# A two-layer transformer trunk on one core: the opening's loads, its first norm factors and one more weight block are laid out anew

## The chip, the core and the metric

The kernel runs on one core of a Trainium2 chip. The metric is the device time of one execution in microseconds (us); lower is better. TensorE (PE in the rows) multiplies, VectorE (DVE), ScalarE (ACT) and GpSimd (POOL) do the rest, and SyncE (SP) issues nearly all DMAs, in one queue. Each engine works through its own instructions strictly in order and waits on semaphores for the others.

## What is computed

A token matrix `x` of 256 x 1024 goes through two layers of three parts: a gated feed-forward block (FFN), an attention mixer, a second FFN. Each part is wrapped in a norm whose shift, scale and gate come from a modulation row:

```python
c_act = jax.nn.silu(c)
mod = (c_act @ ada_w[l] + ada_b[l])[:, None, :]      # 1024 -> 9 x 1024, one row
h = rmsnorm(x, norm_pre[l, 0]) * (1.0 + sc1) + sh1
y = (jax.nn.silu(h @ w_gate) * (h @ w_up)) @ w_down  # 1024 -> 2816 -> 1024
x = x + 0.5 * g1 * rmsnorm(y, norm_post[l, 0])
```

All of it is float32. Of the modulation, the first FFN needs only the shift and scale (`sh1`, `sc1`, columns 0 to 2047 of `ada_w[0]`, 8 MB) before it can start.

## The kernel before

**Products.** Every float32 weight block (1 MB, 128 x 2048) is loaded into a `raw` buffer (3 of them), then split in `unit`: ACT writes the rounded `hi` (6 buffers), DVE writes `lo = raw - hi` (5 buffers), piece by piece; `split=4` makes pieces of 512 columns, `split=8` of 256. The activations are split in the same way into `hT[0]` and `hT[1]`. A product is then three matmuls: `hi*hi`, `hi*lo`, `lo*hi` (`mm3`, lines 487 to 489, 512 columns each; `mm2t`, lines 496 and 499, a pair of 512 and 256 columns).

**Stages.** A section is one FFN or one mixer; six follow each other, with a norm at each seam (`post_norm`, `pre_norm`). Within an FFN, `first` or two "solo" blocks give hidden columns 0 to 511; the loop over `j` (0 to 8) does 256 columns of gate and up at a time; `down` units (11) trail it by `lag`, and at least `tail` of them run behind the loop. Beside this runs the background modulation (`ada_part`, DVE line 524), 512 KB at a time, for later sections.

**The opening.** The first norm needs the modulation, so it is done by quarters q of 256 columns of `h`. For each q: two loads of `ada_w` (1 MB each, s = shift, c = scale, line 929), 16 narrow matmuls (line 991) into `parts`, the bias added on DVE (line 994), a matmul with `sel` that copies the row to all partitions (line 995), two DVE steps for each half of the tokens (lines 1003 and 1004, `gained` at 976 ahead of them), transposes (line 616) and the split of `h` (lines 619, 620). Then the `first` block of this quarter (gate and up columns 0 to 511, 1 MB) is multiplied: 24 matmuls of 512 columns. `START_ORDER` gives the order in which the loads are written: s and c the modulation, x the tokens, g the gain row of `norm_pre` (loaded 128 times over, 256 KB), f the first block. `warm` puts matmuls into the queue whose result is never read (line 969, four passes of 512 columns).

**Norm factors.** `rstd_of` takes the mean square from ACT and makes its inverse root on POOL in two steps: a sum with EPS (line 595) and a power (line 597).

**The order.** `keep_order` at the end models all instructions (costs, the gaps `READY`, priorities shifted by the `START_` and `SEC` numbers) and fixes the order on every engine. Its numbers set order only.

Of the kernel before, what the change touches and what calls it, by code (L numbers as in the profile page):

```python
# [29 lines left out]
START_MM, START_CONV, START_CHAIN, START_SMALL = 590, 826, -286, 74  # L30
START_ORDER = ['s0 x0 s1 c0 g0 x1 c1 f0 s2 f1', 'c2 g1 f2 s3 c3 f3', '', '', '']
WARM = [2, 5, 2]
SEC = [
    dict(plan=('3542', 20, 3), tail=1, lag=1, split=4, sum=-921, dma=-218),
    dict(plan=('76', 9, 4), mix='0011002103011010110011', split=4, sum=-57, dma=24),
    dict(plan=('a8b', 20, 5), tail=4, lag=-1, split=8, sum=353, dma=194),
    dict(plan=('4325', 30, 0), tail=3, lag=1, split=4, sum=-423, dma=-500),
    dict(plan=('67', 8, 3), mix='0000121030111011001011', split=4, sum=473, dma=-406),
    dict(plan=('8', 14, 1), tail=3, lag=2, split=4, sum=-97, dma=-346),
# [4 lines left out]
READY = {("SP", "DVE"): 3600, ("SP", "PE"): 3700, "SP": 3510, ("PE", "DVE"): 290, "PE": 200, ("DVE", "PE"): 235,  # L44
         "DVE": 200, ("Activation", "PE"): 275, "Activation": 145, "Pool": 60}
AFTER = {"SP": 0, "PE": 0, "DVE": 125, "Activation": 100, "Pool": 90}
FBI, BSLACK, FSLACK = 4, {'DVE': 60, 'Activation': 40}, {'DVE': 370, 'Activation': 810}
# [34 lines left out]
def keep_order(tc, nc, slots, shifts):  # L82
# [10 lines left out]
    dur = [cost(i, e, slots) for i, e in zip(L, eng)]  # L93
    prio = list(range(N))
# [60 lines left out]
    def forward(prio):  # L155
# [33 lines left out]
        for _ in range(10 * N):  # L189
# [50 lines left out]
            for j in succs[k]:  # L240
                npred[j] -= 1
                gap = AFTER[e] if eng[j] == e and not dma[k] else READY.get((e, eng[j]), READY[e])
                ready[j] = max(ready[j], end + gap if preds[j][k] else start)
                if not npred[j]:
                    offer(j)
# [7 lines left out]
    def backward(at_, reuse):  # L253
# [16 lines left out]
        while True:  # L270
# [8 lines left out]
            for j, kind in ps[k].items():  # L279
                nsucc[j] -= 1  # L280
                if kind is True:
                    gap = AFTER[eng[j]] if eng[j] == e and not dma[j] else READY.get((eng[j], e), READY[eng[j]])
                else:
# [23 lines left out]
def trunk(ctx, tc, x, c, rel_bias, ada_w, ada_b, norm_pre, norm_post, w_gate, w_up,  # L307
# [74 lines left out]
    nc.vector.memset(mhalf, -0.5)  # L382
    xs = [ctile([P, D], f"x{h}") for h in range(2)]
# [56 lines left out]
    def unit(key, shape, src, uses=1):  # L440

        if key not in units:
# [3 lines left out]
            for z in range(sec["split"]):  # L446
                sl = slice(z * 2048 // sec["split"], (z + 1) * 2048 // sec["split"])
                nc.scalar.activation(hi[:, sl], raw[:, sl], AF.Copy)  # L448
                nc.vector.tensor_sub(lo[:, sl], raw[:, sl], hi[:, sl].bitcast(F32))  # L449
            units[key] = [uses, hi.rearrange("p (a b) -> p a b", a=shape[0]),  # L450
                          lo.rearrange("p (a b) -> p a b", a=shape[0])]
# [233 lines left out]
    def ffn(l, i, first):  # L685
# [21 lines left out]
        for j in range(9):  # L707
# [4 lines left out]
            gu = []  # L712
            for b, (tag, ws) in enumerate((("g", w_gate), ("u", w_up))):
                w = u_both(l, f, ws, tag, j)
                gu.append(st())
                for t in range(2):
                    p_ = wps(b)
                    mm2t(p_, KT, w, slice(t * P, (t + 1) * P))
                    dst = gu[b][:, t * 256:(t + 1) * 256]
                    nc.scalar.activation(dst, p_[:, 256:], AF.Copy)  # L720
                    nc.vector.tensor_add(dst, p_[:, :256], dst)  # L721
            nc.scalar.activation(gu[0], gu[0], AF.Silu)
            nc.vector.tensor_mul(gu[0], gu[0], gu[1])
            act = split(gu[0], 512)
# [201 lines left out]
    def ada_load(m, q):  # L926

        raw = (plo if m else phi).tile([P, KT, 256], F32, tag="lo" if m else "hi", name=nm("eraw"))
        nc.sync.dma_start(raw, rows(ada_w[0], 0, KT)[:, :, m * D + q * 256:m * D + (q + 1) * 256])
        return raw  # L930
# [4 lines left out]
    def load_gain(n):  # L935
        grow[n] = stage()
        nc.sync.dma_start(grow[n], norm_pre[0, 0:1, n * 512:(n + 1) * 512].to_broadcast([P, 512]))

    def load_first(q):
        loaded["first", q] = load((4, 512), first_srcs(q))  # L940

# [16 lines left out]
    def start_load(order):  # L958
        for w in order.split():
            {"s": lambda q: load_mod(q, 0), "c": lambda q: load_mod(q, 1), "x": load_x, "g": load_gain,  # L960
             "f": load_first}[w[0]](int(w[1]))
# [8 lines left out]

    warm(WARM[0], gb)
    rx, xg = [None, None], [[None, None], [None, None]]
# [58 lines left out]
    keep_order(tc, nc, slots, shifts)  # L1031
# [48 lines left out]
```

## Time and profile before

| | |
|---|---|
| three runs, median (lowest to highest) | 1021.07 us (1020.7 to 1021.27) |
| profiled execution, its own time | 1020.83 us |
| its span in the profile | 1019.0 us |
| busy share of the span: PE, DVE, ACT, POOL | 98%, 84%, 59%, 4% |
| moved by DMA | 261.82 MB, 257 GB/s mean |

The 1.8 us between the profiled execution's time and its span lie outside the instructions. A matmul's "busy" time is longer than its share of the engine, since matmuls are pipelined; the distance from one start to the next is what one costs. `x16` on line 991 is 8 instructions: a float32 matmul has two records.

### The profile page before, as it was taken

What the parts mean: (1) busy time and instruction counts of PE and PEld (TensorE: products, weight loads), DVE (VectorE), ACT (ScalarE), POOL (GpSimd) and SP (SyncE); (2) the same over time, 40 slices, a digit from 0 to 9 for tenths busy, and PEclk for the clock granted to TensorE, in tenths of its full rate; (3) what the DMA queues carried; (4) which work ended last, traced back from release to release, by engine and by line L of the source; (5) the groups of instructions that cost most, each with busy time, mean ns of one, the idle gap of its engine ahead of it and who ended that gap; (6) DMA issues with size and microseconds to landing.
All of it is one profiled execution on the core that took longest, in us unless ns stands there. A gap on an engine that the chain in (4) does not pass through costs nothing. (4 is left out here: it accounts for less than half of the span.)

```text
span 1019.0 us, 15260 instructions
## 1 busy us (share of the span) xinstructions
PE 999.0 (98%) x5362; PEld 833.0 (82%) x5362; DVE 852.3 (84%) x1637; ACT 600.0 (59%) x1394; POOL 44.2 (4%) x92
## 2 busy tenths in 40 slices
PE   8999999999999999999999999999999999999997
PEld 3588888887888888888878888888888788888886
DVE  4799999988987998899789999987878898666652
ACT  3256555664677675667465566655477666655541
POOL 1000000011001000000020000000100110000000
PEclk9999999999999999999999999999999999999999
DMA  9999899857995588888549999977689747655511
GB/s 332 367 340 328 304 308 342 307 197 230 334 315 191 185 288 280 281 288 297 203 164 319 323 324 311 311 258 244 195 296 295 242 144 264 206 173 200 182 66 42
DMA packets 171848, 261.82 MB, mean 257 GB/s; under 512 B 6396, under 2 KB 107484, under 8 KB 171772
## 3 DMA queue, kind: packets, MB, share of 16 engines
q1 hardware_dynamic: 171616, 260.78, 75.9%
q8 instruction: 42, 0.69, 0.3%
q14 instruction: 34, 0.28, 0.1%
q10 hardware_dynamic: 156, 0.07, 0.0%
HBM read 259.76 MB, written 1.07 MB: 256 GB/s over the span
## 5 line engine op out<-in xcount | busy, mean ns | idle before, releaser
L449 DVE TENSOR_TENSOR lo_a<-raw_a,hi_a 128x512 fp32r<-128x512 f32 (+1 forms) x540 | 296.6, 593 | 37.1 <-PE w_b L499 10.8
L448 ACT ACTIVATE hi_a<-raw_a 128x512 fp32r<-128x512 f32 (+1 forms) x540 | 261.1, 548 | 52.6 <-DMA raw_a<-in_ffn_w_up_dram 16.2
L496 PE MATMUL w_a<-hT,hi_a 128*128 128x512 f32 x640 | 223.9, 397 | 0.0
L496 PE MATMUL w_b<-hT,hi_b 128*128 128x512 f32 x512 | 179.4, 397 | 0.0
L499 PE MATMUL w_a<-hT,lo_a 128*128 128x256 f32 x640 | 166.6, 281 | 0.0
L496 PEld LDWEIGHTS w_a<-hT,hi_a 128*128 128x128 f32 x640 | 116.7, 188 | 22.7 <-DVE str_a L660 0.2
L449 DVE TENSOR_TENSOR lo_b<-raw_b,hi_b 128x512 fp32r<-128x512 f32 (+1 forms) x224 | 121.0, 589 | 15.5 <-PE w_a L499 7.2
L499 PE MATMUL w_b<-hT,lo_b 128*128 128x256 f32 x512 | 132.9, 281 | 0.0
L499 PEld LDWEIGHTS w_a<-hT,lo_a 128*128 128x128 f32 x640 | 120.8, 189 | 7.1
L448 ACT ACTIVATE hi_b<-raw_b 128x512 fp32r<-128x512 f32 (+1 forms) x224 | 106.2, 544 | 20.8 <-DMA raw_b<-in_ffn_w_up_dram 7.6
L496 PEld LDWEIGHTS w_b<-hT,hi_b 128*128 128x128 f32 x512 | 93.7, 188 | 18.7 <-issue 0.6
L499 PEld LDWEIGHTS w_b<-hT,lo_b 128*128 128x128 f32 x512 | 96.6, 189 | 5.9
L524 DVE SCALAR_TENSOR_TENSOR acc_a<-araw_a,ccol,acc_a 128x512 f32<-128x512 f32 x110 | 82.2, 747 | 2.3 <-DMA araw_a<-in_ada_w_dram 0.7
L720 ACT ACTIVATE st_a<-w_a 128x256 f32<-128x256 f32 x80 | 30.4, 383 | 76.7 <-PE w_a L496 75.7
L720 ACT ACTIVATE st_b<-w_b 128x256 f32<-128x256 f32 x64 | 24.1, 384 | 64.1 <-PE w_b L496 63.8
L487 PE MATMUL a_b<-hi_a,str_a 128*128 128x512 f32 x156 | 60.9, 391 | 0.0
L488 PE MATMUL a_b<-lo_a,str_a 128*128 128x512 f32 x156 | 60.8, 391 | 0.0
L489 PE MATMUL a_b<-hi_a,str_a 128*128 128x512 f32 x156 | 60.4, 390 | 0.0
L721 DVE TENSOR_TENSOR st_a<-w_a,st_a 128x256 f32<-128x256 f32 x80 | 33.3, 421 | 16.6 <-ACT st_a L720 16.3
L595 POOL TENSOR_SCALAR rstd_a<-ss_a 128x1 f32<-128x1 f32 x13 | 6.6, 511 | 721.0 <-ACT junk L645 694.4
L487 PE MATMUL w_a<-hi_a,hT 128*128 128x512 f32 (+1 forms) x96 | 36.6, 381 | 0.6 <-DVE hT L620 0.6
L507 PE MATMUL w_a<-hT,hi_a 128*128 128x256 f32 x128 | 37.0, 292 | 0.0
(255 smaller groups left out, 1930.0 us busy)
## 6 DMA issues: line engine op xcount, KB each, us to landing
araw_a<-in_ada_w_dram SPq DMA_DIRECT2D x84, 512.0 KB
raw_a<-in_ffn_w_down_dram SPq DMA_DIRECT2D x30, 1024.0 KB
raw_a<-in_ffn_w_gate_dram SPq DMA_DIRECT2D x26, 1024.0 KB
raw_a<-in_ffn_w_up_dram SPq DMA_DIRECT2D x26, 1024.0 KB
araw_b<-in_ada_w_dram SPq DMA_DIRECT2D x44, 512.0 KB
raw_a<-in_mix_w_in_dram SPq DMA_DIRECT2D x18, 1024.0 KB
raw_b<-in_ffn_w_gate_dram SPq DMA_DIRECT2D x16, 1024.0 KB
raw_b<-in_ffn_w_up_dram SPq DMA_DIRECT2D x16, 1024.0 KB
```

What stands on the lines that cost most here:

```text
L448: nc.scalar.activation(hi[:, sl], raw[:, sl], AF.Copy)
L449: nc.vector.tensor_sub(lo[:, sl], raw[:, sl], hi[:, sl].bitcast(F32))
L487: nc.tensor.matmul(ps_, hh, wh, start=start, stop=False)
L488: nc.tensor.matmul(ps_, hh, wl, start=False, stop=False)
L489: nc.tensor.matmul(ps_, hl, wh, start=False, stop=stop)
L496: both = lambda **f: nc.tensor.matmul(ps_, wh, hTa[:, kt], **f)
L499: nc.tensor.matmul(ps_[:, :256], wl, hT[0][:, kt], start=False, stop=False)
L507: nc.tensor.matmul(ps_, wh, hh, start=start, stop=False)
L524: nc.vector.scalar_tensor_tensor(acc[:, :n], raw[:, t, :], ccol[:, k:k + 1], b if t == 0 else acc[:, :n], op0=ALU.mult, op1=ALU.add)
L595: nc.gpsimd.tensor_scalar(r, s0, 1.0 if s1 is None else s1, EPS, op0=ALU.mult if s1 is None else ALU.add, op1=ALU.add)
L720: nc.scalar.activation(dst, p_[:, 256:], AF.Copy)
L721: nc.vector.tensor_add(dst, p_[:, :256], dst)
```

## The change

- **Loads.** For the first quarter the shift and the scale columns come as two loads of 512 KB each. A new load b (`load_next`) brings, by quarters of 512 KB, the gate and up weights of the loop's block `j = 0`.
- **Products.** In each quarter 24 matmuls of 256 columns on this block stand with the first block's (lines 1057 to 1059), into PSUM tiles `ahead`; `ffn` then takes `j = 0` from there.
- **Bias and gain.** In quarter 0 the bias goes into `both` by a product of one row (line 1016), the two halves of `parts` are copied by ACT and DVE (line 1024) and spread apart (line 1025). The gain row is loaded once (2 KB, ACT's queue) and spread by a product of one row (line 957).
- **Norm factors.** `rstd_of` adds EPS and the two sums on ACT (lines 605, 608); the power stays on POOL (line 609).
- **Numbers.** The two last `warm` matmuls go; `lag`, `tail`, `split`, the plans of the background work and the planner's gaps change in most sections: `split` 4 to 8 in the fourth and fifth, `lag` 1 to 2 in the first and fourth, `tail` 4 to 5 in the third.

```diff
-START_ORDER = ['s0 x0 s1 c0 g0 x1 c1 f0 s2 f1', 'c2 g1 f2 s3 c3 f3', '', '', '']
-WARM = [2, 5, 2]
+START_ORDER = ['g0 x0 s0 c0 f0 x1 b0 s1 c1 f1 b1 g1 s2', 'c2 f2 b2 s3', 'c3 f3 b3', '', '']
+WARM = [2, 5, 0]
-    dict(plan=('3542', 20, 3), tail=1, lag=1, split=4, sum=-921, dma=-218),
+    dict(plan=('3542', 19, 6), tail=1, lag=2, split=4, sum=-921, dma=-218),
...
-    dict(plan=('4325', 30, 0), tail=3, lag=1, split=4, sum=-423, dma=-500),
-    dict(plan=('67', 8, 3), mix='0000121030111011001011', split=4, sum=473, dma=-406),
+    dict(plan=('4325', 31, 1), tail=3, lag=2, split=8, sum=-859, dma=-502),
+    dict(plan=('67', 9, 4), mix='0000121030111011001011', split=8, sum=680, dma=-406),
...
-        r, r2 = tiny(1, tag), tiny(1, tag + "2")
-        nc.gpsimd.tensor_scalar(r, s0, 1.0 if s1 is None else s1, EPS, op0=ALU.mult if s1 is None else ALU.add,
-                                op1=ALU.add)
-        nc.gpsimd.tensor_tensor(r2, r, mhalf, op=ALU.pow)
-        return r2
+        r = tiny(1, tag)
+        e = eps
+        if s1 is not None:
+            e = tiny(1, tag + "e")
+            nc.scalar.activation(e, s0, AF.Identity, bias=eps)
+            s0 = s1
+        v = tiny(1, tag + "v")
+        nc.scalar.activation(v, s0, AF.Identity, bias=e)
+        nc.gpsimd.tensor_tensor(r, v, mhalf, op=ALU.pow)
+        return r
...
+            if q == 0:
+                nc.tensor.matmul(both, sel[0:1, :], fl(brow0[0:1, 0]), start=True, stop=False)
...
+                if q == 0:
+                    (nc.vector.tensor_copy if z else nc.scalar.copy)(t[:, zc], parts[:, zc])
+                    nc.tensor.matmul(both[:, zc], sel, t[:, zc], start=False, stop=z == 1)
...
+        with shift(START_CONV):
+            w = unit(("next", q), (4, 256), None, 1)
+        with shift(START_NEXT):
+            for n in range(2):
+                for t in range(2):
+                    for k in range(2):
...
+                        nc.tensor.matmul(p_, wh, hT[0][:, kt], start=kt == t == 0, stop=False)
+                        nc.tensor.matmul(p_, wh, hT[1][:, kt], start=False, stop=False)
+                        nc.tensor.matmul(p_, wl, hT[0][:, kt], start=False, stop=kt == 7 and t == 1)
```

Three places show how instructions move. First, TensorE in the first quarter, before (`a_b` is the filler's target, `eraw` a modulation block, `x_120` the second half of the tokens):

```order
L969 MATMUL a_b_137<-x_119,ident 128x512 x4
L991 MATMUL w_a_202<-eraw_a_147,ccol 32x256 x8
L991 MATMUL w_a_202<-eraw_a_152,ccol 32x256 x8
L995 MATMUL w_a_203<-st_a_220,str_a_138 128x512
L969 MATMUL a_b_137<-x_120,ident 128x512
L616 MATMUL w_a_226<-ident,st_a_223 128x128
L991 MATMUL w_a_289<-eraw_a_150,ccol 32x256 x6
```

and after:

```order
L1021 MATMUL w_a_224<-eraw_a_155,ccol 32x256 x4
L1016 MATMUL w_a_225<-erow_a_146,str_a_140 128x512
L1021 MATMUL w_a_224<-eraw_a_158,ccol 32x256 x8
L1025 MATMUL w_a_225<-st_a_226,str_a_140 128x256
L994 MATMUL a_b_139<-x_121,ident 128x512
L1025 MATMUL w_a_225<-st_a_226,str_a_140 128x256
```

The filler on `x_120` ahead of the first transpose is gone, and no matmul of quarter 1 stands between the two transposes of quarter 0 any more; fillers on `x_121`, the first half of the tokens, stand between the pieces.

Second, SyncE's queue at the start, before:

```order
L933 DMA x_119<-in_x_dram 128x1024
L929 DMA eraw_a_152<-in_ada_w_dram 128x8x256
L929 DMA eraw_a_147<-in_ada_w_dram 128x8x256
L929 DMA eraw_a_150<-in_ada_w_dram 128x8x256
L937 DMA str_a_154<-in_norm_pre_dram 128x512
L933 DMA x_120<-in_x_dram 128x1024
L437 DMA raw_a_159<-in_ffn_w_gate_dram 128x2x512
L929 DMA eraw_a_157<-in_ada_w_dram 128x8x256
```

and after:

```order
L951 DMA x_121<-in_x_dram 128x1024
L947 DMA eraw_a_158<-in_ada_w_dram 128x4x256
L947 DMA eraw_a_155<-in_ada_w_dram 128x4x256 x2
L947 DMA eraw_a_158<-in_ada_w_dram 128x4x256
L951 DMA x_122<-in_x_dram 128x1024
L443 DMA raw_a_161<-in_ffn_w_gate_dram 128x2x512
L443 DMA raw_a_165<-in_ffn_w_gate_dram 128x2x256
L443 DMA raw_a_161<-in_ffn_w_up_dram 128x2x512
L443 DMA raw_a_165<-in_ffn_w_up_dram 128x2x256
```

The first quarter's two blocks come in four pieces, the second half of the tokens and the first blocks stand ahead of the second quarter's modulation, and `raw_a_165` is the new block.

Third, TensorE in quarter 2, from the spreading matmul (line 995) to the transposes (line 616), before:

```order
L995 MATMUL w_a_361<-st_a_378,str_a_138 128x512
L489 MATMUL a_b_137<-hi_a_318,hT 128x512
L616 MATMUL w_a_386<-ident,st_a_383 128x128 x2
L991 MATMUL w_a_435<-eraw_a_282,ccol 32x256 x8
L487 MATMUL a_a_134<-hi_a_391,hT 128x512
```

and after (line 1028 spreads, line 628 transposes):

```order
L1028 MATMUL w_a_458<-st_a_459,str_a_140 128x512
L1059 MATMUL w_a_198<-hT,lo_a_416 128x256
L496 MATMUL a_a_137<-hi_a_373,hT 128x512
L494 MATMUL a_b_138<-hi_a_373,hT 128x512
L495 MATMUL a_b_138<-lo_a_374,hT 128x512
L496 MATMUL a_b_138<-hi_a_373,hT 128x512
```

One product stood there before; ten stand there now (one of 256 and nine of 512 columns), of which the first five are shown.

## Rows read from the trace of the kernel before

**Rows 1.** Windows: busy us (and instructions) by engine, granted clock, DMA share, GB/s.

```profile
core 0: us, PE busy (x) PEld busy (x) DVE busy (x) ACT busy (x) POOL busy (x), PEclk, DMA share, GB/s
0.00:10.00 10.00, 7.34 (x14) 3.27 (x15) 2.71 (x6) 2.92 (x6) 2.63 (x13) 1.00 0.83 276
10.00:20.00 10.00, 8.03 (x54) 2.78 (x55) 4.31 (x8) 1.97 (x6) 0.87 (x2) 0.83 1.08 366
20.00:30.00 10.00, 10.00 (x62) 6.45 (x64) 6.96 (x15) 4.12 (x9) 0.00 (x0) 1.00 1.07 376
30.00:40.00 10.00, 8.86 (x58) 5.20 (x50) 7.64 (x12) 2.30 (x4) 0.00 (x0) 1.00 1.09 358
40.00:50.00 10.00, 9.10 (x62) 5.38 (x61) 8.31 (x17) 3.71 (x7) 0.00 (x0) 1.00 1.07 370
...
60.00:222.00 162.00, 162.00 (x841) 137.34 (x840) 153.56 (x258) 98.54 (x200) 1.60 (x3) 1.00 0.93 319
524.00:712.00 188.00, 187.34 (x963) 158.53 (x962) 172.95 (x287) 107.70 (x216) 4.74 (x8) 1.00 0.85 289
```

**Rows 2.** Timeline, first quarter: start, busy us, engine, line, idle before and its releaser.

```profile
7.13 3.70 PE L969 MATMUL a_b<-x,ident 128*128 128x512 f32 x8
...
13.79 1.10 PE L995 MATMUL w_a<-st_a,str_a 128*128 128x512 f32 x2 [0.90 <-DVE st_a L994]
...
19.99 0.38 ACT L619 ACTIVATE hT<-w_a 128x256 fp32r<-128x256 f32 x1 [2.12 <-PE w_a L616]
...
21.00 0.79 PE L487 MATMUL a_a<-hi_a,hT 128*128 128x512 f32 x1
```

**Rows 3.** Timeline: paces of PE: eight of line 991, then 512 and 256 columns.

```profile
22.17 1.07 PE L991 MATMUL w_a<-eraw_a,ccol 128*32 128x256 f32 x16
...
23.17 0.50 PE L487 MATMUL a_b<-hi_a,hT 128*128 128x512 f32 x1
...
25.98 0.39 PE L488 MATMUL a_a<-lo_a,hT 128*128 128x512 f32 x1
...
26.89 0.39 PE L488 MATMUL a_a<-lo_a,hT 128*128 128x512 f32 x1
...
226.49 0.28 PE L487 MATMUL w_a<-hi_a,hT 128*128 128x256 f32 x1
...
226.97 0.28 PE L488 MATMUL w_a<-lo_a,hT 128*128 128x256 f32 x1
```

**Rows 4.** Timeline, quarter 2: the step on DVE and the transposes behind it.

```profile
40.54 0.42 DVE L1004 TENSOR_TENSOR st_a<-st_a,w_a 128x256 f32<-128x256 f32 x1
...
41.11 0.41 PE L616 MATMUL w_a<-ident,st_a 128*128 128x128 f32 x2 [0.83 <-DVE st_a L1004]
```

**Rows 5.** Timeline: the first block's last matmul, then block 0 of the loop.

```profile
56.56 0.39 PE L489 MATMUL a_b<-hi_a,hT 128*128 128x512 f32 x1
...
57.58 0.40 PE L496 MATMUL w_a<-hT,hi_a 128*128 128x512 f32 x1
...
57.93 0.40 PE L496 MATMUL w_a<-hT,hi_a 128*128 128x512 f32 x1
...
59.73 0.66 PE L682 MATMUL w_b<-ident,st_b 128*128 128x128 f32 x4 [0.70 <-DVE st_b L666]
```

**Rows 6.** Groups by line and form, DVE: the low parts of the weights.

```profile
L449 DVE TENSOR_TENSOR lo_a<-raw_a,hi_a 128x512 fp32r<-128x512 f32 x356 | 229.3, 684 | 32.7 <-PE w_a L499 9.8 <-PE w_b L499 8.6 <-ACT hi_a L448 7.9
L449 DVE TENSOR_TENSOR lo_a<-raw_a,hi_a 128x256 fp32r<-128x256 f32 x184 | 67.3, 417 | 4.5 <-PE w_b L499 2.2 <-ACT hi_a L448 2.0
```

**Rows 7.** Groups by form: POOL's norm factors, a tiny ACT step; timeline: a seam.

```profile
L595 POOL TENSOR_SCALAR rstd_b<-ss_b 128x1 f32<-128x1 f32 x11 | 7.4, 670 | 34.2 <-ACT junk L645 23.9 <-ACT junk L625 7.9 <-DVE st_b L635 2.2
L597 POOL TENSOR_TENSOR rstd_b<-rstd_b,mhalf 128x1 f32<-128x1 f32 x11 | 6.3, 576 | 0.8
L414 ACT ACTIVATE bq<-w_b 128x8 f32<-128x8 f32 x1 | 0.2, 178 | 0.2 <-PE w_b L412 0.2
...
230.89 0.33 PE L750 MATMUL w_a<-ident,st_a 128*128 128x128 f32 x1 [1.36 <-DVE st_a L797]
```

More of the change, by code (lines that the diff above doesn't have):

```diff
@@ L93, in keep_order @@
     dur = [cost(i, e, slots) for i, e in zip(L, eng)]
+    lag = [LATE[k >= at[calm]] if d else 0 for k, d in enumerate(dma)]
     prio = list(range(N))
@@ L242, in forward @@
                 gap = AFTER[e] if eng[j] == e and not dma[k] else READY.get((e, eng[j]), READY[e])
[L243 removed]
+                ready[j] = max(ready[j], end + gap + lag[k] if preds[j][k] else start)
                 if not npred[j]:
@@ L282, in backward @@
                     gap = AFTER[eng[j]] if eng[j] == e and not dma[j] else READY.get((eng[j], e), READY[eng[j]])
+                    gap += lag[j]
                 else:
@@ L711, in ffn @@
                     setup_table(*small)
[L712 to L724, printed above, removed]
+            if first and j == 0:
+                hm = swiglu(*ahead)
+            else:
+                gu = []
+                for b, (tag, ws) in enumerate((("g", w_gate), ("u", w_up))):
+                    w = u_both(l, f, ws, tag, j)
+                    gu.append(st())
+                    for t in range(2):
+                        p_ = wps(b)
+                        mm2t(p_, KT, w, slice(t * P, (t + 1) * P))
+                        dst = gu[b][:, t * 256:(t + 1) * 256]
+                        nc.scalar.activation(dst, p_[:, 256:], AF.Copy)
+                        nc.vector.tensor_add(dst, p_[:, :256], dst)
+                nc.scalar.activation(gu[0], gu[0], AF.Silu)
+                nc.vector.tensor_mul(gu[0], gu[0], gu[1])
+                hm = gu[0]
+            act = split(hm, 512)
             for h in range(2):
@@ L928, in ada_load @@
         raw = (plo if m else phi).tile([P, KT, 256], F32, tag="lo" if m else "hi", name=nm("eraw"))
-        nc.sync.dma_start(raw, rows(ada_w[0], 0, KT)[:, :, m * D + q * 256:m * D + (q + 1) * 256])
+        n = KT // 2 if q == 0 else KT
+        for k in range(0, KT, n):
+            nc.sync.dma_start(raw[:, k:k + n], rows(ada_w[0], k * P, n)[:, :, m * D + q * 256:m * D + (q + 1) * 256])
         return raw
@@ L936, in load_gain, with load_next @@
         grow[n] = stage()
-        nc.sync.dma_start(grow[n], norm_pre[0, 0:1, n * 512:(n + 1) * 512].to_broadcast([P, 512]))
+        nc.scalar.dma_start(grow[n][0:1], norm_pre[0, 0:1, n * 512:(n + 1) * 512])
+        p_ = wps(n)
+        nc.tensor.matmul(p_, sel[0:1, :], grow[n][0:1], start=True, stop=True)
+        nc.scalar.activation(grow[n], p_, AF.Copy)
     def load_first(q):
         loaded["first", q] = load((4, 512), first_srcs(q))
+    def load_next(q):
+        loaded["next", q] = load((4, 256), [(slice(n * 2, n * 2 + 2), rows(w[0, 0], q * 256, 2)[:, :, 512:768])
+                                            for n, w in ((0, w_gate), (1, w_up))])
     def load_mod(q, m):
```

45 lines of the change are left out of this document (29 added, 16 removed).

## The prediction

> **What bounds the kernel now.** I read the windows first [rows 1]. The reader is to see two regimes. From 60 to 222 us PE has no idle time at all and DVE is busy 153.56 of 162 us; the same holds, nearly, from 524 to 712. There the time is PE's, and only fewer or cheaper matmuls could shorten it. From 0 to 50 us the DMA share is 1.07 to 1.09 from the second row on and PE idles: 30 to 50 us alone lose 2.0 us of plain idle, and a pipelined matmul hides more. So the opening is set by what has landed and by a chain of small steps, and a microsecond gained there is a microsecond of the total, provided that later stages follow.
>
> The timeline shows the first chain [rows 2]: PE runs filler from 7.13, spreads the first modulation at 13.79 after waiting for DVE, the first `hT` is written at 19.99, and the first real product starts at 21.00. The granted clock is 0.83 on average from 10 to 20 us [rows 1]: a part of it ran at the lower of the two levels, 1.2 instead of 2.4 GHz, after PE had idled. The opening's product is complete at 56.56 + 0.23 = 56.8 [rows 5].
>
> **The paces.** From start to start [rows 3]: a product of 512 columns costs (26.89 - 25.98) / 4 = 0.2275 us, one of 256 (226.97 - 226.49) / 4 = 0.12, eight of line 991 1.0 us (22.17 to 23.17). A four-pass float32 matmul of 512 columns (lines 995, 969) is four times the first, 0.91. A transpose of 128 columns is at most 0.12.
>
> **Before, from its first product on.** 35.8 us pass from 21.0 to 56.8. In them: 96 products, 21.8; five groups of line 991, 5.0; three spreading matmuls, 2.7; 14 transposes, 1.7; together 31.2. The waits are therefore 4.6 us. After that come block 0's 32 pairs at 57.93 - 57.58 = 0.35, 11.2 us, and a wait of 0.70 [rows 5]. So before has "first block and block 0 done" at 56.8 + 11.2 + 0.7 = 68.7 us (eight transposes of line 682 stand on both sides and are left out).
>
> **After: the first product.** By the order, PE does between 7.13 and the first quarter's transposes: one gain spread, five fillers and the bias product, seven at 0.91, 6.4; two groups of modulation, 2.0; two halves of a spread, 0.9. That ends at 16.4. The modulation of quarter 0 with x, 2.62 MB, lands by about 10 us (276 GB/s by 10 us, 2.76 MB [rows 1]), so PE's own queue sets this, not the DMA; the half pieces matter little, and no row shows less. Two DVE steps of 0.42 with hops of 0.15 (40.54 + 0.42 to 41.11 [rows 4]) add 1.1: 17.5. A last filler lies beneath them. Two transposes and a hop, 0.4; then `hT` and, behind it on ACT now, the first `hi` piece: the 1.0 us from 19.99 to 21.00 [rows 2]. First product at **19.0**. Bounds: 17.8 if the gain spread finds its place in PE's idle time before 7.13 and the chain's hops overlap; 20.7 if PE falls to 1.2 GHz again over two fillers (2 x 0.91). I take the value between, nearer the lower: fillers leave PE no gap in which the clock fell before.
>
> **After: from there on.** Work: 96 products of 512, 21.8; 96 of 256, 11.5 (block 0 costs 0.3 more than as pairs); six groups of modulation, 6.0; three spreads, 2.7; transposes, 1.7; sum 43.7. Would the data be there? x, modulation, first block and block 0 are 1.05 + 8.39 + 4.19 + 2.10 = 15.7 MB, with two background pieces ahead 16.8. The windows deliver 2.8, 6.4, 10.2, 13.8 and 17.5 MB by 10, 20, 30, 40 and 50 us [rows 1], so all of it is in at 48 us, ahead of PE. Each quarter brings 3.67 MB, 9.9 us at 370 GB/s, and 10.9 us of PE work (43.7 / 4): DMA and PE are matched, PE a little slower. Block 0's low parts are 16 pieces of 0.366 on DVE (67.3 / 184 [rows 6]), 5.9 us, which the 7.1 us that DVE idled from 20 to 50 cover [rows 1]; without that cover they would cost up to 5.9.
>
> The waits: before, PE waited 0.83 us for the transposes of quarter 2 [rows 4], with one product in front of them; now ten products (2.2 us) stand there, more than the 1.1 us of DVE steps, and likewise behind each modulation group. What stays is the start of quarter 1, whose modulation is later in the queue: 6.8 MB, landing at 21 us, and low parts that DVE has not yet made. Bounds: 0, and 4.6 as before; I take 1.6, nearer the lower, since every place where a filled-in product stands is now longer than its chain. Done at 19.0 + 43.7 + 1.6 = 64.3: **4.4 us earlier**.
>
> **Does the rest follow?** The next gate block ends at 18.9 MB of the queue, about 54 us, 10 us before PE wants it. Fewer background sums stand ahead of it on DVE (by the order, 8 against 20 ahead of that block), so DVE is ahead, and pays these later, where it had 8.4 us idle from 60 to 222 [rows 1].
>
> **The norm factors.** POOL's first step takes 0.67 us on average in the second half, the power 0.576, and a tiny ACT step 0.18 [rows 7]. One of the two ACT steps runs ahead, so a chain gets up to 0.49 shorter. PE waits at seams, for 1.36 us at one [rows 7]; there DVE stood behind such a chain. Five seams with one deciding chain: 2.4 at most; part is hidden, I take **1.5**. Bounds: a loss of 0.5 (the ACT steps queue behind splits), a gain of 3.4 (with a larger `lag` or `tail`, another unit's 12 products, 2.7 us, cover the seam of the other half).
>
> The POOL step of 0.67 stands beside DVE instructions that read two operands from SBUF (`raw` and `hi` of line 449). The Trainium skill (SBUF — State Buffer, "SBUF: two separate sides") says that such a DVE operation and a GpSimd operation that reads SBUF share a port pair by exclusive lock, and the later one blocks. The trace agrees as far as it goes, 0.67 against the smaller power step. It speaks against the term: the power that stays on POOL reads SBUF too.
>
> **Smaller pieces.** In the fourth section 33 units are split by 256: each pair costs 2 x 0.366 - 0.644 = 0.088 us more on DVE [rows 6], 132 pairs, 11.6 us. DVE idled 188 - 172.95 = 15.05 us there [rows 1]. That hides it; priced at nothing, it is a rival. The fifth section adds 4.6 us where DVE is less loaded.
>
> **Sum**, against the profiled execution's 1020.83 (0.24 below the median): 1020.8 - 4.4 - 1.5 = **1014.9**.
>
> **The rivals.**
> - Waits return: PE's queue is in order, and each group of the second modulation waits for its landing. Waits 4.6, seams 0.5: 1020.8 - 1.4 - 0.5 = 1018.9. For it: before, work filled only 31.2 of 35.8 us. Against: ten products in place of one.
> - POOL's power inherits the wait at the seams: 1020.8 - 4.4 = 1016.4. For it: 0.67 stands beside DVE's splits. Against: the power behind it averages only 0.576 [rows 7], though it stands among the same splits. By the rule of the Trainium skill (SBUF — State Buffer) on the lock this is the case.
> - Everything fits: first product 17.8, no wait (gain 7.2), seams 3.4: 1010.2. For it: 48 us against 64 in the landings.
> - Slower: in the fourth section DVE, at 92% before, goes to 98%, and its idle time is made of waits that cannot be filled. If none is usable, 11.6 are lost: it decides once less than 5.7 of the 15 us are usable; at a third or less usable, about 9 lost, 1020.8 - 5.9 + 9 = 1024. Against: from 60 to 222 DVE ran at 95% and PE never idled [rows 1].
> - The opening doesn't do what it says: the first product stays at 21 or later, because fillers now stand inside the chain and the clock falls, and what block 0 fills in comes out of nothing: 1020.8.
>
> **How the numbers follow.** Chances: forecast 0.42, everything fits 0.17, power inherits 0.13, waits return 0.14, no effect 0.08, slower 0.06. The time is the forecast's, 1014.9; its own range is 1012 to 1017.5. The range goes down to 1010.3, half of "everything fits" left out, and up to 1019.2, past "waits return"; out are no effect and slower: 0.22 in all, about 2 in 10. A measurement can tell 0.2%, 2 us, from no change. "Waits return" lies on that edge, half and half: faster 0.42 + 0.17 + 0.13 + 0.07 = 0.79, same 0.07 + 0.08 = 0.15, slower 0.06.
>
> **What would show it.** In the profile after: the first product of the first block at 19 us and no window below 0.95 clock from 10 to 20 us; the last product of first block and block 0 at 64 us; the DMA share still above 1.0 to about 48 us; no POOL sum, tiny ACT steps, and seam waits of PE shorter by a few tenths each; DVE near 98% from 520 to 700 with PE still without idle. Wrong: a first product at 21, PE idle above 5 us between 19 and 64, or PE waiting for low parts in the fourth section.

## The result, and the profile after

The changed kernel takes 1013.92 us (median of six runs, 1012.7 to 1014.21) against 1020.77 for the kernel before (six runs, 1020.45 to 1021.27): a ratio of 0.993 with a 95% interval of 0.9918 to 0.9943. The forecast was 1014.9, the range 1010.3 to 1019.2. The time is right, but by luck: the opening brought 1.0 us instead of 4.4 and the rest of the kernel 5.6 instead of 1.5, and the two errors nearly cancel.

The windows of the kernel after, in the order of [rows 1]: busy us and instructions by engine, granted clock, DMA share, GB/s.

```profile
0.00:10.00 10.00, 6.90 (x8) 2.27 (x9) 2.89 (x8) 4.27 (x10) 2.31 (x12) 1.00 0.78 262
10.00:20.00 10.00, 10.00 (x47) 3.59 (x46) 1.01 (x2) 2.42 (x8) 0.55 (x1) 1.00 1.08 368
20.00:30.00 10.00, 8.89 (x66) 5.98 (x68) 8.18 (x17) 5.22 (x12) 0.00 (x0) 1.00 1.09 359
30.00:40.00 10.00, 10.00 (x79) 6.43 (x70) 6.70 (x15) 4.32 (x11) 0.00 (x0) 1.00 1.08 364
40.00:50.00 10.00, 10.00 (x70) 7.60 (x66) 6.85 (x13) 3.44 (x10) 0.00 (x0) 1.00 0.88 296
...
524.00:712.00 188.00, 188.00 (x970) 159.69 (x970) 177.15 (x413) 122.31 (x359) 2.83 (x4) 1.00 0.82 276
```

From 30 to 50 us TensorE has no idle time left where it had 2.0 us. In the fourth section DVE is busy 177.15 of 188 us, not the 98% foreseen, and TensorE is never idle. But the row of 10 to 20 us deceives: TensorE is busy for all of 10 to 20 us with 47 instructions, and the printed clock is 1.00. The trace records the first level of the clock only at 14.10 us; ahead of the first record the view prints 1.00. The durations show the level. These are TensorE's rows of the first quarter after:

```profile
2.76 2.04 PE L994 MATMUL a_b<-gb,ident 128*128 128x512 f32 x2 [2.76 <-DMA ident<-in_ident_dram]
5.14 2.04 PE L957 MATMUL w_a<-str_a,str_a 1*128 1x512 f32 x2 [0.34 <-DMA str_a<-in_norm_pre_dram]
...
7.05 2.05 PE L957 MATMUL w_a<-str_a,str_a 1*128 1x512 f32 x2
9.03 2.08 PE L994 MATMUL a_b<-gb,ident 128*128 128x512 f32 x2
10.90 3.48 PE L994 MATMUL a_b<-x,ident 128*128 128x512 f32 x4
14.31 0.64 PE L1021 MATMUL w_a<-eraw_a,ccol 128*32 128x256 f32 x8
14.88 1.13 PE L994 MATMUL a_b<-x,ident 128*128 128x512 f32 x2
...
22.95 0.51 PE L494 MATMUL a_a<-hi_a,hT 128*128 128x512 f32 x1 [0.99 <-ACT hi_a L455]
```

Up to 14 us a float32 matmul of 512 columns (two rows of the trace) takes 1.7 to 2.1 us, and from 14.88 on 1.13: until 14.1 us TensorE ran at 1.2 GHz, then at 2.4. In the kernel before, the trace has it at 2.4 GHz from 5.84 us on, with the fall of [rows 1] from 16.08 to 19.49. The one-row products that spread the norm gain (`1*128` in the rows) and the fillers behind them stood ahead of line 1021 at half the clock, though the modulation was there: in a kernel below (all rows, same plan) its first products run at 9.98 us without a wait. So the first product came at 22.95 us, later than the 21.00 of [rows 2].

The end of the opening, to set beside [rows 5]: the kernel before with the last pair of block 0, then the kernel after with the last product of the first block.

```profile
70.73 0.40 PE L496 MATMUL w_a<-hT,hi_a 128*128 128x512 f32 x1
70.97 0.40 PE L488 MATMUL a_b<-lo_a,str_a 128*128 128x512 f32 x1
```

```profile
67.86 0.40 PE L496 MATMUL a_b<-hi_a,hT 128*128 128x512 f32 x1
68.09 0.60 PE L694 MATMUL w_a<-ident,st_a 128*128 128x128 f32 x4
```

Before, block 0 ends at 70.97; four products of other work (0.93 us) and two groups of transposes of line 682 (0.35 and 0.61) stand within it, so like for like it is 69.1 (the prediction had 68.7). After it is 68.09. The opening gained 1.0 us.

What TensorE waited for between 70 and 1015 us, engine and line first, then us in total, times, longest: the kernel before, then the kernel after.

```profile
PE w_a L750 <- DVE st_a L797: 2.2, 2, 1.4
PE w_b L616 <- DVE st_b L638: 1.0, 3, 0.5
PE w_a L616 <- DVE st_a L638: 0.8, 2, 0.4
PE w_b L616 <- DVE st_b L875: 0.6, 1, 0.6
PE w_a L487 <- DVE hT L620: 0.6, 1, 0.6
PE w_b L847 <- ACT st_b L841: 0.5, 3, 0.2
PE a_a L856 <- ACT st_a L849: 0.5, 1, 0.5
```

```profile
PE w_a L766 <- DVE st_a L813: 1.2, 2, 0.8
PE w_b L628 <- DVE st_b L650: 0.7, 2, 0.4
PE w_a L494 <- DVE hT L632: 0.3, 1, 0.3
PE w_a L863 <- ACT st_a L857: 0.2, 1, 0.2
```

6.2 us became 2.4. The wait of [rows 7] is the largest of both kernels and fell from 1.4 to 0.8.

**A table for the whole kernel.** To see where time went I walked TensorE's rows: at each matmul of the work proper (no fillers, spreads or modulation) its start, less the paces of all such matmuls before it (0.2275, 0.12 and, for a pair, 0.3525, near those of [rows 3, 5]; a transpose 0.109, other shapes by the median of their rows). That is the time lost so far. The table says by how much each kernel is later than the changed kernel at the same amount of work. The places: when the opening is over (40 us of work), after the first seam, in the first mixing section's second half, after the third and the fourth seam, at the end.

| kernel | opening | seam 1 | mixing | seam 3 | seam 4 | end |
|---|---|---|---|---|---|---|
| before | 1.3 | 2.2 | 2.9 | 3.4 | 4.8 | 6.9 |
| factors alone, on before | 2.3 | 2.1 | 2.9 | 3.6 | 3.8 | 4.3 |
| factors back | 0.5 | 1.7 | 1.9 | 2.8 | 3.6 | 7.6 |
| sections back | 1.9 | 2.8 | 3.8 | 3.9 | 5.4 | 6.1 |
| planned anew, DVE | 0.3 | 2.5 | 3.3 | 3.4 | 3.6 | 5.0 |
| planned anew, GpSimd | 0.3 | 0.0 | -0.8 | -0.7 | -0.7 | 1.0 |
| longer factor, same plan | -0.2 | 0.4 | 0.3 | 0.9 | 1.4 | 2.9 |
| full rows, same place | -3.1 | -3.1 | -3.5 | -3.5 | -3.5 | -2.6 |
| gain over all rows, same plan | -4.2 | -4.3 | -4.9 | -4.9 | -4.9 | -5.0 |

The end of the first row, 6.9, less the 0.24 us by which block 0 is dearer in single products (96 at 0.12 against 32 pairs at 0.3525), is the 6.7 us between the two spans (1019.0 and 1012.3). Of the 6.9, 1.3 is won in the opening (the 1.0 above and the dearer block 0) and 5.6 behind it: 0.8 at the first seam, 0.8 in the first mixing section, 0.5 from there to the third seam, 1.4 at the fourth, 2.1 in the second mixing section and at the last seam. Kernels whose order is the same differ by up to 0.9 us in one profiled execution each (the last two rows change by 0.5 and 0.8 after the opening with nothing changed there), so I read nothing smaller than 1 us from it.

### The profile page after: what moved, and what is told of

Read it like the earlier page. It is cut to its first block, busy times and chain, and to the rows that moved or that the text cites. A ratio compares the mean times of both kernels' runs of the same rounds, so it can differ in the third digit from the quotient of the medians.

```text
span 1012.3 us, 15724 instructions
## 1 busy us (share of the span) xinstructions
PE 999.4 (99%) x5398; PEld 835.3 (83%) x5398; DVE 859.1 (85%) x1826; ACT 630.5 (62%) x1641; POOL 31.1 (3%) x60
## 4 chain that ended last, share of the span: by engine, by line
issue 56%; PE 37%; DVE 3%; DMA 2%; POOL 1%; ACT 1%; ACTq 0%; POOLq 0%; DVEq 0%
PE w_b L503 3%; PE w_a L503 3%; PE a_b L494 3%; PE a_b L495 2%; PE a_b L496 2%; PE w_a L506 1%; PE w_b L506 1%; PE a_b L872 1%; PE w_b L848 1%; PE a_a L494 1%; PE w_a L514 1%; PE w_a L516 1%; PE w_a L515 1%; PE a_a L495 1%; PE a_a L496 1%
## 5 line engine op out<-in xcount | busy, mean ns | idle before, releaser
L456 DVE TENSOR_TENSOR lo_a<-raw_a,hi_a 128x256 fp32r<-128x256 f32 (+1 forms) x684 | 307.0, 499 | 27.6 <-PE w_b L506 8.9
L455 ACT ACTIVATE hi_a<-raw_a 128x256 fp32r<-128x256 f32 (+1 forms) x684 | 275.4, 472 | 50.2 <-PE a_b L496 14.3
L503 PE MATMUL w_a<-hT,hi_a 128*128 128x512 f32 x608 | 212.7, 397 | 0.0
L506 PE MATMUL w_a<-hT,lo_a 128*128 128x256 f32 x608 | 158.4, 281 | 0.0
L456 DVE TENSOR_TENSOR lo_b<-raw_b,hi_b 128x256 fp32r<-128x256 f32 (+1 forms) x272 | 125.4, 511 | 15.5 <-PE w_a L506 7.1
L455 ACT ACTIVATE hi_b<-raw_b 128x256 fp32r<-128x256 f32 (+1 forms) x272 | 111.4, 482 | 16.3 <-DMA raw_b<-in_ffn_w_up_dram 7.3
L494 PE MATMUL a_b<-hi_a,str_b 128*128 128x512 f32 x132 | 51.4, 389 | 0.0
L495 PE MATMUL a_b<-lo_a,str_b 128*128 128x512 f32 x132 | 51.3, 389 | 0.0
L496 PE MATMUL a_b<-hi_a,str_b 128*128 128x512 f32 x132 | 51.3, 389 | 0.0
L494 PE MATMUL a_b<-hi_a,str_a 128*128 128x512 f32 x108 | 42.3, 391 | 0.0
L495 PE MATMUL a_b<-lo_a,str_a 128*128 128x512 f32 x108 | 42.1, 390 | 0.0
L496 PE MATMUL a_b<-hi_a,str_a 128*128 128x512 f32 x108 | 41.9, 391 | 0.0
```

The source lines that it names most:

```text
L494: nc.tensor.matmul(ps_, hh, wh, start=start, stop=False)
L495: nc.tensor.matmul(ps_, hh, wl, start=False, stop=False)
L496: nc.tensor.matmul(ps_, hl, wh, start=False, stop=stop)
L503: both = lambda **f: nc.tensor.matmul(ps_, wh, hTa[:, kt], **f)
L506: nc.tensor.matmul(ps_[:, :256], wl, hT[0][:, kt], start=False, stop=False)
```

## Experiments on the opening

**Full rows in the same place.** The question is whether the one-row products held the clock down, or whether something else did. This kernel leaves out the norm gain; its first spread comes ahead of the first filler, and all other instructions keep their order on every engine.

```diff
-        nc.tensor.matmul(p_, sel[0:1, :], grow[n][0:1], start=True, stop=True)
+        nc.tensor.matmul(p_, ident, gb, start=True, stop=True)
```

> The changed kernel with the two one-row products that spread the norm gain replaced by two products over all 128 rows (ident by gb) in the same place; every other instruction stands in the same order. It leaves out the norm gain of the opening's input, so its numbers aren't the reference's. Theory C, the one-row products between the fillers keep the granted clock at its lower level until 14.1 us: now the clock is full from 5.5 to 7 us on, the five fillers take 0.43 us each pass, line 1021 begins at about 10.5 to 11.5 us instead of 14.3, the first product at 19.5 to 21 us instead of 22.95, and the whole is 1010.5 to 1013 us. Theory D, the clock rises late for another reason (it rises as late, at about 14 us) or the first product then waits for x and the weights just as long: 1013.4 to 1014.4 us.

1011.3 us (1011.1 to 1011.53), ratio to before 0.9906 (0.9892 to 0.9919). TensorE's rows, in the columns of the timeline:

```profile
2.71 2.05 PE L957 MATMUL w_a<-gb,ident 128*128 128x512 f32 x2 [2.71 <-DMA ident<-in_ident_dram]
...
6.60 2.08 PE L957 MATMUL w_a<-gb,ident 128*128 128x512 f32 x2
8.47 1.06 PE L994 MATMUL a_b<-gb,ident 128*128 128x512 f32 x2
...
11.18 0.64 PE L1021 MATMUL w_a<-eraw_a,ccol 128*32 128x256 f32 x8
...
19.82 0.50 PE L494 MATMUL a_a<-hi_a,hT 128*128 128x512 f32 x1 [0.99 <-ACT hi_a L455]
```

The filler at 8.47 takes 1.06 us, the same filler at 9.03 of the changed kernel 2.08. The trace has full clock from 8.55 us. Everything from line 1021 to the end of the opening moved by 3.1 us as one block: first product 19.82 instead of 22.95. Theory C holds, though the clock rose later than its 5.5 to 7 us.

**The gain spread over all rows.** Its row lands in a zeroed buffer, and the product takes all 128 rows.

```diff
+        nc.vector.memset(grow[n], 0.0)
         nc.scalar.dma_start(grow[n][0:1], norm_pre[0, 0:1, n * 512:(n + 1) * 512])
...
-        nc.tensor.matmul(p_, sel[0:1, :], grow[n][0:1], start=True, stop=True)
+        nc.tensor.matmul(p_, sel, grow[n], start=True, stop=True)
```

> The changed kernel with the norm gain spread by products over all 128 rows: its row lands in a buffer that is zero elsewhere, and the product takes all rows of it. The planner then puts both gb fillers and three x fillers first and the two spreads after them. Theory C (one-row products between the fillers keep the clock low): full clock from 6 to 9 us on, line 1022 from 10.5 to 11.5 us, first product at 19.5 to 21 us, 1010.5 to 1013 us. Theory D (something else): clock full at about 14 us and 1013.4 to 1014.5 us. If another plan costs by itself, the loss shows after 70 us and the first product is early all the same.

1012.05 us (1011.14 to 1012.72), ratio 0.991 (0.9895 to 0.9926). Full clock from 6.88 us, line 1022 at 10.32, but first product only at 20.48: TensorE stood still for 1.63 us ahead of the transposes at 19.44, and the clock fell to half from 20.53 to 23.94 us. Of the early start 1.4 us were left at the end of the opening. So far theory C, in a kernel whose order is another one.

**And with two fillers fewer.** The same kernel with `WARM = [2, 3, 0]`.

> As the kernel with the gain spread over all rows, and two fillers fewer on x (3 instead of 5), so that none stands inside the first chain. Theory I, fillers at full clock cost their time in the chain (0.85 us each): first product 1 to 2 us earlier than with five, 1009.5 to 1012 us. Theory J, they keep the clock: with three it falls to half ahead of the first product, which then comes no earlier, and the whole is 1012 to 1015 us.

1013.67 us (1012.57 to 1014.54), ratio 0.9925 (0.9913 to 0.9938): nothing over the changed kernel. TensorE's wait ahead of the transposes is 3.12 us (16.6 to 19.75), and the clock is at half from 18.08 to 24.90 us. A row of VectorE, and the one of TensorE that waits:

```profile
16.89 0.75 DVE L1003 SCALAR_TENSOR_TENSOR str_b<-x,rstd_a,str_a 128x512 f32<-128x512 f32 x1 [2.87 <-POOL rstd_a L609]
...
19.75 0.69 PE L628 MATMUL w_a<-ident,st_a 128*128 128x128 f32 x2 [3.12 <-DVE st_a L1038]
```

The time is that of theory J, but the fillers did not set it. In this kernel and the one before, VectorE's new order has a step for the second half of the tokens (`str_b`, from 16.89 and from 16.51 us, waiting for that half's norm factor) ahead of the first half's last steps, and the transposes wait for these until 19.75 and 19.44 us. So TensorE's queue was not the limit, and what the two fillers are worth is not shown here.

**All rows, and the same plan.** Here the buffer is zeroed by GpSimd, and the planner counts that as nothing, so DVE and ACT keep every row in its place, and TensorE all but the first few.

```diff
+        nc.gpsimd.memset(grow[n], 0.0)
         nc.scalar.dma_start(grow[n][0:1], norm_pre[0, 0:1, n * 512:(n + 1) * 512])
...
-        nc.tensor.matmul(p_, sel[0:1, :], grow[n][0:1], start=True, stop=True)
+        nc.tensor.matmul(p_, sel, grow[n], start=True, stop=True)
```

> The changed kernel with the norm gain spread by products over all 128 rows (its row lands in a buffer that GpSimd has set to zero), VectorE's and ACT's rows all in the same place and TensorE's but for six of the first ones. Theory C (one-row products keep the clock low, and a clock that is full early carries through the opening): full clock from 6 to 9 us, first product at 19.5 to 20.5 us, no fall behind it, the same plan after the opening: 1010.8 to 1012 us. Theory D': the early gain is given back by a fall of the clock at 18 to 25 us, as in the two kernels with other plans (3.4 and 6.8 us at the lower level): 1012 to 1013.5 us.

1010.28 us (1009.07 to 1010.72), ratio 0.989 (0.9876 to 0.9903): faster than the kernel before and the changed one. Full clock from 5.94 us, and no fall behind it; theory C asked for less (19.5 to 20.5 us for the first product, which stands at 18.62).

```profile
2.72 3.55 PE L997 MATMUL a_b<-gb,ident 128*128 128x512 f32 x4 [2.72 <-DMA ident<-in_ident_dram]
...
7.32 1.88 PE L960 MATMUL w_a<-str_a,str_a 128*128 128x512 f32 x4
...
9.98 0.64 PE L1024 MATMUL w_a<-eraw_a,ccol 128*32 128x256 f32 x8
...
18.62 0.50 PE L496 MATMUL a_a<-hi_a,hT 128*128 128x512 f32 x1 [0.99 <-ACT hi_a L457]
```

**Narrow fillers.** The same with the first three fillers on x at 128 columns, which the planner counts as before.

```diff
-            nc.tensor.matmul(first[1][1], ident, src, start=True, stop=True)
+            c = 128 if n == 5 and i < 3 else 512
+            nc.tensor.matmul(first[1][1][:, :c], ident, src[:, :c], start=True, stop=True)
```

> As the one before, with the first three of the five fillers on x cut to 128 columns of 512, the last two left, all in the same place. Theory I, the fillers ahead of the first chain's products cost their time: some 0.75 us less for each of them at full clock, 2 us at most, first product at 18 to 19.5 us, 1009.5 to 1011 us. Theory J, the clock rises later or falls once more for want of them, and the first product comes no earlier: 1011 to 1013.5 us.

1008.78 us (1008.34 to 1010.61), ratio 0.9883 (0.9868 to 0.9898): the fastest, though its interval overlaps with that of the kernel before it. First product at 17.21, clock full from 7.04 us without a fall. Theory I: fillers ahead of the chain's own products cost their time. The first product comes 1.41 us earlier, and 0.8 of that is left at the end of the opening. The two fillers beneath the DVE steps were left as they are, so nothing is shown of them.

**Without block 0 in the opening.** Its loads, products and conversions are left to the loop; the diff takes out `load_next`, the letters b and the block under `START_NEXT`.

> The changed kernel without block 0's quarters in the opening: block 0 comes after the first block, as before. First product at about 23 us as in the changed kernel. Theory G, the quarters fill TensorE's waits of the opening: between the first product and the end of block 0 it waits 3 to 5 us more, and the whole is 1016.5 to 1019 us. Theory H, these waits were set by the transfers and would come back after the opening: 1013.9 to 1015 us.

1016.17 us (1015.86 to 1016.62), ratio 0.9952 (0.9938 to 0.9966), between the two theories. At the end of the opening it is 4.0 us behind the changed kernel: 1.65 are there at the first product already (24.60 against 22.95), and the clock fell to half from 25.33 to 28.74, which is 1.7 more. After 24.6 us the trace shows no wait of TensorE in the opening at all. So the waits of 3 to 5 us that block 0 was to fill did not come back as waits. By the end of the kernel 2.4 of the 4.0 us are left. This kernel has another order and a fall of the clock, so what the block itself is worth can't be told from it.

## Experiments on the rest

**Factors alone.** The kernel before with the new `rstd_of` and nothing else of the change.

```diff
-        nc.gpsimd.tensor_scalar(r, s0, 1.0 if s1 is None else s1, EPS, op0=ALU.mult if s1 is None else ALU.add,
-                                op1=ALU.add)
-        nc.gpsimd.tensor_tensor(r2, r, mhalf, op=ALU.pow)
+            nc.scalar.activation(e, s0, AF.Identity, bias=eps)
+        nc.scalar.activation(v, s0, AF.Identity, bias=e)
+        nc.gpsimd.tensor_tensor(r, v, mhalf, op=ALU.pow)
```

> The kernel before with only the new norm factors (the two sums with Epsilon on ACT, the power on GpSimd), nothing of the opening or of the sections' numbers. After the opening the changed kernel loses about 5.3 us less time on TensorE than the kernel before (6.9 us less in all, 1.3 of it by 68 us). Theory A, the factors give most of that, in the ten chains at the seams and the eight chains of gated outputs: 1015.5 to 1017.5 us. Theory B, the sections' numbers (how far ahead w_down runs, its tail, which adaLN chunks run where, the parts of a split) give it: 1019.3 to 1020.8 us, the waits of TensorE at line 750 and 616 within 0.4 us of those of before.

1018.18 us (1017.41 to 1018.59), ratio 0.9972 (0.9961 to 0.9982). By the table it loses 1.0 in the opening (another plan, and the clock at half from 34.88 to 38.30 us) and wins 3.6 behind it. More than B, less than A.

**Factors back**, the reverse diff on the changed kernel.

> The changed kernel with the old norm factors (both steps on GpSimd) put back, everything else as changed. Theory A (factors give the 5.3 us after the opening): 1017.5 to 1019.5 us. Theory B (the sections' numbers give them): 1013.9 to 1015.2 us.

1020.33 us (1019.73 to 1021.82), ratio 0.9997 (0.9988 to 1.0006): more than A asked for, 7.1 us lost after the opening.

**Sections back.** The six rows of `SEC` as before, in the changed kernel.

> The changed kernel with the six rows of numbers of the sections (chunk plan, tail, lag, split, sum, dma) of the kernel before, opening and factors as changed. Theory A (factors): 1013.5 to 1015 us. Theory B (sections' numbers): 1016.5 to 1019 us, with the waits at the seams and in the two mixing sections as long as before.

Median 1019.77 us, above theory B's range, but four runs lie at 1017.46 to 1017.73 and seven at 1019.2 to 1021.08 (the profiled one at 1020.21); ratio 0.9983 (0.9974 to 0.9992). 1.9 us are lost in the opening, where the clock fell from 23.44 to 26.85 us, and 4.2 after it. Together the two parts would be worth 7.1 + 4.2 = 11.3 us after the opening, twice what was won there. So they are not two shares of one gain; either the two parts need each other, or something else costs time whenever one is put back. The next kernel asks for the second.

**Planned anew.** Both kernels had another order, since the planner orders whatever it is given. How much does another order cost by itself? Here nothing is undone; a single gap of the planner is 130 ns in place of 125.

```diff
-AFTER = {"SP": 0, "PE": 0, "DVE": 125, "Activation": 100, "Pool": 90}
+AFTER = {"SP": 0, "PE": 0, "DVE": 130, "Activation": 100, "Pool": 90}
```

> The changed kernel, with every instruction of it and none undone; only the planner is told that a result of DVE is ready for DVE 130 ns after it instead of 125. That alone moves 376 of TensorE's 5193 rows and 871 of VectorE's 1829 (the kernel with the old factors had 513 and 665 moved). Theory E, the sections' numbers are fitted to one plan and another plan of the same program loses most of the 4 to 7 us that the two kernels with a part put back lost after the opening: 1016.5 to 1020 us. Theory F, another plan costs little and those losses belong to the factors and to the sections' numbers: 1013 to 1015 us.

1019.75 us (1018.95 to 1021.42), ratio 0.9988 (0.9979 to 0.9996): 5.8 us slower for nothing. 2.2 are lost at the first seam. DVE there, planned anew, and below it the same in the changed kernel:

```profile
214.35 1.54 DVE L531 SCALAR_TENSOR_TENSOR acc_a<-araw_a,ccol,acc_a 128x512 f32<-128x512 f32 x2
215.80 0.68 DVE L662 TENSOR_TENSOR st_a<-a_b,row_a 128x512 f32<-128x512 f32 x1
...
226.37 0.68 DVE L632 TENSOR_TENSOR hT<-w_a,hT 128x512 fp32r<-128x512 f32 x1
```

```profile
214.25 0.69 DVE L662 TENSOR_TENSOR st_a<-a_b,row_a 128x512 f32<-128x512 f32 x1 [0.60 <-ACT junk L657]
...
224.44 0.68 DVE L632 TENSOR_TENSOR hT<-w_a,hT 128x512 fp32r<-128x512 f32 x1
```

Two background sums (line 531) stand ahead of the chain's first step, which starts 1.55 us later, and the first `hT` comes at 226.37 instead of 224.44. TensorE's two waits there, in the kernel planned anew:

```profile
227.11 0.39 PE L494 MATMUL w_a<-hi_a,hT 128*128 128x256 f32 x1 [1.77 <-DVE hT L632]
...
232.03 1.32 PE L628 MATMUL w_b<-ident,st_b 128*128 128x128 f32 x8 [1.54 <-DVE st_b L650]
```

The first is for that `hT`. The second is for a step of VectorE that begins no later than before (231.22 against 231.48); but the changed kernel has line 766 and twelve products of 512 columns in front of those transposes, and this one has them behind.

**Planned anew, a second time**, with GpSimd's results 75 ns late in the planner's count instead of 60.

> The changed kernel, none of it undone; the planner is told that a result of GpSimd is ready after 75 ns instead of 60. That moves 196 of TensorE's 5193 rows and 318 of VectorE's 1829. Theory E (any other plan of these numbers loses at the seams): 1015.5 to 1020 us. Theory F' (the first such kernel was an unlucky plan): 1013.2 to 1015 us.

1014.75 us (1013.88 to 1015.21), ratio 0.9935 (0.9922 to 0.9947): as the changed kernel and as theory F' had it. So neither E nor F alone: orders of the same instructions differ by nothing or by 5 us. What a kernel with another order loses can't be put down to its edit.

**A longer factor in the same plan.** This has no such flaw: ACT's last step of each factor takes 317 columns in place of one, the planner counts it as before, and no row moves.

```diff
-        nc.scalar.activation(v, s0, AF.Identity, bias=e)
+        nc.scalar.activation(wide, s0.to_broadcast([P, 317]), AF.Identity, bias=e)
```

> The changed kernel with ACT's last step of every norm factor made longer by some 0.26 us (317 columns in place of one, 316/1.2 ns) and no instruction in another place on any engine. It is the factor's price by itself, with no other plan. Theory K, each norm chain ends a wait of TensorE, so the length of a factor shows at the end: 20 chains at the seams times 0.26 us would be 5.3 us if every one counted, and the share that counts is what the new factor is worth; with a third to a half of them, 1015.5 to 1016.7 us. Theory L, the plan has work behind the chains and their length hardly counts: 1013.5 to 1014.6 us, and the 3.6 us after the opening that the factors alone won on the kernel before were mostly another plan's.

1017.75 us (1017.26 to 1018.61), ratio 0.9966 (0.9953 to 0.9978). The step, by groups (count, busy us, mean ns): the changed kernel, then this one.

```profile
L608 ACT ACTIVATE rstdv_a<-ss_a,rstde_a 128x1 f32<-128x1 f32 x13 | 3.8, 295 | 0.8
```

```profile
L609 ACT ACTIVATE wide<-ss_a,rstde_a 128x317 f32<-128x317 f32 x13 | 7.3, 561 | 1.1
```

0.266 us more in each of the 30 chains after the opening are 8.0 us; by the table 3.1 of them show (-0.2 at the opening, 2.9 at the end; the medians, each set against the kernel before measured beside it, differ by 3.2). So about 0.38 us of each us in this step reaches the end, give or take 0.1 by the table's 1 us. Theory K, beyond its 1015.5 to 1016.7 us.

## Why the prediction was right, and where it was not

- **First product at 19.0: failed, by 3.95 us.** The step that failed is PE's own queue: 9.3 us were priced from 7.13 to the end of the spread, and 13.3 passed (7.05 to 20.38). The steps behind it were right, 2.6 us priced and 2.57 measured. The working asked whether TensorE falls to 1.2 GHz again and allowed 20.7 for it. It did not ask when it rises. The prediction priced "one gain spread, five fillers and the bias product" at 0.91 us each; up to 14 us they took 1.7 to 2.1. With full rows in the same place the first product stood at 19.82, so 3.13 of the 3.95 us are the two one-row products and the level that went with them. With the spread over all rows and the same plan, where one filler fewer stands behind 7.13, it came at 18.62; but then the time was 1010.28, 4.6 us under the forecast.
- **From the first product on: right.** 43.7 + 1.6 = 45.3 us were forecast, and 68.09 - 22.95 = 45.1 passed. But the 1.4 us over the 43.7 are no plain waits: behind the 0.99 us ahead of the first product the trace shows no wait of TensorE in the opening. The DMA share fell below 1.0 in the window from 40 us on, not at 48.
- **The rival "the opening doesn't do what it says"** had the first half of what happened there: first product later than 21, by the clock and by the fillers inside the chain. Its second half was wrong: from the first product on 45.1 us passed where it was 69.1 - 21.0 = 48.1, so what block 0 fills in brought 3.0. It had 0.08.
- **The norm factors: the size fits, the reasons don't.** A tiny ACT step takes 0.285 to 0.295 us, not 0.18. At a seam's second norm neither step runs ahead, and the power is longer. Two such chains, each from ACT's last read of the sums, the kernel before and the changed one:

```profile
710.70 0.19 ACT L625 ACTIVATION_READ_ACCUMULATOR junk<-x 128x1 f32 x1
...
710.98 0.88 POOL L595 TENSOR_SCALAR rstd_a<-ss_a 128x1 f32<-128x1 f32 x1 [2.46 <-ACT junk L625]
711.94 0.56 POOL L597 TENSOR_TENSOR rstd_a<-rstd_a,mhalf 128x1 f32<-128x1 f32 x1
```

```profile
706.63 0.19 ACT L637 ACTIVATION_READ_ACCUMULATOR junk<-x 128x1 f32 x1
...
706.72 0.28 ACT L605 ACTIVATE rstde_a<-ss_a,eps 128x1 f32<-128x1 f32 x1
707.09 0.29 ACT L608 ACTIVATE rstdv_a<-ss_a,rstde_a 128x1 f32<-128x1 f32 x1
707.09 1.09 DVE L456 TENSOR_TENSOR lo_a<-raw_a,hi_a 128x256 fp32r<-128x256 f32 x3
707.47 1.12 POOL L609 TENSOR_TENSOR rstd_a<-rstdv_a,mhalf 128x1 f32<-128x1 f32 x1 [2.95 <-ACT rstdv_a L608]
```

  From the end of that read it is 1.61 us before (710.89 to 712.50) and 1.77 after (706.82 to 708.59): this chain is longer. The power's mean in its two largest groups is 756 and 827 ns against the 576 of [rows 7], so the rival "POOL's power inherits the wait" was right in part. The Trainium skill (SBUF — State Buffer, "SBUF: two separate sides") has GpSimd and an operation of DVE with two inputs from SBUF share a port pair by exclusive lock; the trace agrees here: the power of 1.12 us begins in the middle of three splits on DVE, which read `raw` and `hi`, and ends 0.41 us after the last of them. It is so throughout: 17 of the 32 powers of the changed kernel take 0.59 to 1.31 us, and each of these ends 0.41 us after an operation of VectorE with two operands from SBUF (lines 456, 531, 647); the other 15 take 0.55 to 0.57. Such a chain's end is VectorE's, and a longer step ahead of it need not show. The same chain with the longer factor, whose read ends at 708.22:

```profile
708.49 1.09 DVE L458 TENSOR_TENSOR lo_a<-raw_a,hi_a 128x256 fp32r<-128x256 f32 x3
...
709.13 0.85 POOL L610 TENSOR_TENSOR rstd_a<-wide,mhalf 128x1 f32<-128x1 f32 x1 [3.22 <-ACT wide L609]
```

  It ends at 709.98, after 1.76 us, although its ACT step is 0.27 longer. Over all 32 chains, from the end of ACT's last read of the sums to the end of the power, the sum went from 44.5 us before to 41.0 after: 0.11 us for each, not 0.49. But far more than five chains count: at 0.38 the 3.5 us would be worth some 1.3, near the 1.5 of the forecast. That is an estimate, as it takes all chains alike; the 3.6 us that the factors alone won came with another order.
- **The rest of the gain, some 4 us, had no term.** The sections' numbers were priced at nothing, with a larger `lag` or `tail` only in the bound, and the two mixing sections were not named although 2.9 of the 5.6 us were won in them and at the last seam, right behind the second. How far these 4 us belong to the numbers themselves, and how far to the choice of one good order among those that the planner can make, stays open: another order of the same instructions cost 5.8 us once and none once.
- **The fourth section: right that nothing shows there.** Low parts rose from 85.3 to 93.7 us of DVE in the window, not by 11.6, and 3.7 us of background sums moved out of it. TensorE waited for none of it.

The opening brought 3.4 us less than forecast and the rest 4.1 more. The forecast of 1014.9 met the 1014.1 of the profiled execution because these two errors, which have nothing to do with each other, are of about the same size: luck.

## What to carry to other kernels

Price what stands ahead of the first real product at the clock level of that stretch, read from the durations there, and ask of every added filler or small product what TensorE does until the level rises, as well as what may make it fall. Where a planner makes the order, compare edits in kernels whose order is the same, or run the unchanged program in a second order first: here that alone was worth 5.8 us, nearly all of the gain. To price a chain that all parts wait for, lengthen one step by a known time with every instruction in its place, see what share arrives at the end, and look whether the chains themselves end later.

## What was not expected of the hardware

In the seven profiled kernels with no one-row product among the first fillers, the trace has full clock from 5.84 (the kernel before), 5.94, 6.88, 7.04, 7.58, 7.84 and 8.55 us on. In the seven in which the two one-row products stood between the first fillers it is 12.71, 13.2, 13.57, 14.10 (the changed kernel), 14.79, 15.03 and 15.09. TensorE had begun at 2.6 to 3.2 us in all of them and stood still for at most 0.5 us at a time until the clock rose. Within each group the spread of 2.4 to 2.7 us is not explained by any row that I found.

In six kernels the clock fell to half once more within the opening, in five for 3.4 us and in one for 6.8. Three of the six had one wait of TensorE of 1.63, 2.61 and 3.12 us just ahead of the fall or across it (the 6.8 us go with the 3.12), the other three two waits of 0.5 to 1.0 us close to each other; among these is the kernel before, with 0.90 and 0.95. In the eight without a fall, the changed kernel and the two fastest among them, the only wait of that size behind the rise is one of 0.99 us. That it is these waits which decide was not tested.
